# A two-group mixer layer on one core: order of the row scales, the embedding sums, the mixing weight and the gate tiles

## The chip, the core and the metric

The kernel runs on one core of a Trainium2 chip. The metric is the device time of one execution in microseconds. The core has a matrix engine (TensorE, PE in the rows, with its weight loads as PEld), a vector engine (VectorE, DVE), a scalar engine (ScalarE, ACT), a general engine (GpSimd, POOL) and an engine that here only issues DMAs (SyncE, SP). Each engine takes its instructions in one fixed order, and waits on semaphores where an instruction needs what another engine or a DMA makes.

## The reference

One layer (the stack has depth 1) on x of 1024 positions by 1024 features, all in float32:

```
h = rms_norm(x, pre_norm_gain)
q, k, v, z_a, b, c, u, z_c = split(h @ w_in, 8)          # 512 columns each
lam = exp(sum(lq1*lk1)) - exp(sum(lq2*lk2)) + 0.2
# group A: 4 heads, two softmax maps per head, ALiBi bias, block-causal mask
attn = rms_norm((softmax(q1 k1) - lam * softmax(q2 k2)) @ v, subln_gain) * 0.8 * silu(z_a)
# group B: depthwise convolution of width 3
conv = b * conv3(c * u) * silu(z_c)
x = x + rms_norm(concat(attn, conv) @ w_out, post_norm_gain)
e = rms_norm(p @ w_ple_proj, ple_norm_gain)              # p: 1024 by 256
out = x + sigmoid(x @ w_ple_gate) * e
```

## The kernel before

Everything is held transposed, features on the 128 partitions and positions along the free dimension, in two halves of 512 positions. Each float32 matrix product is made of three passes (lines 94 to 96): operands are split into a high part (ScalarE, line 83 or 86) and a low part (VectorE, or GpSimd for most weights, line 84 or 87). A product tile of 128 features by 512 positions takes 24 matmuls of 512 columns.

The order in which each engine gets its instructions is not the order of the text. The program is built with a scheduler that simulates the engines: among the instructions that are ready it prefers what stands earlier in the text, and it fixes one order per engine. A tile pool with a tag hands its few buffers round, so an instruction can also be late because a buffer isn't free.

The stages, with the names that matter here:

- **Embedding.** `embed(n, p)` makes e = p @ w_ple_proj for half n in 8 tiles `ple`, and stores them to DRAM (`e_dram`) through SP. Around it x is loaded (`load_x`), split into `hT`, and the weight tiles `wq`, `wk` of head 0 are loaded.
- **Row scales.** `row_scale(n)` finds 1/rms of x for half n: seven squares on ScalarE (`sqx`) added up on VectorE into `R[n]`, a transpose `flip` and a reduction `part` on VectorE, a small matmul `ms` on TensorE (line 110, in a PSUM bank of tag "t", which the `ple` tiles use too), a power on GpSimd (`rsx`, line 91), and a transpose that spreads the result into `R[n]` (line 114). Four copies then put the same numbers into `r_col`, by which v is scaled. `sqx`, `flip` and the temporaries `tq`, `ql`, `tk` of q and k share three buffers (pool `rowp`, tag "t").
- **Head 0's q, k, z and all of v.** `run` multiplies a weight tile with one half or both, and its evacuation (`ev_q`, `ev_k`, `ev_z`) multiplies the PSUM bank by `R[n]`. Half 1 of q and k has banks of its own (`bank_s`); z and v use the two banks of `bank_p`. v needs `r_col`. In the text `row_scale(1)` stands between the two halves of q and k.
- **Mixing weight.** `mixing_weight()` (lines 156 to 163) loads the four lambda vectors, broadcast over the partitions, into part of a buffer of x (`mix[5][1]`), and needs two products, two reductions, an exponential and two more small operations. In the text it stands behind v.
- **Heads.** For each head the list `PLAN` says the order of the steps: 'a' softmax blocks, 'v' reload v, 'g' `values` (transposes `tpw`, splits `wt`, products `av`, then a square on ScalarE, line 265, and column sums), 'n' `scale_values`, 'c' tiles of the convolution group, which fill TensorE, and 's' `embed_scale(n)` in heads 0 and 1.
- **Embedding sums.** `embed_scale(n)` (lines 429 to 441) reads back the eight tiles of e for half n into `mix[7]`, `mix[6]` and `mix[3]` (the last two in turn), squares each on ScalarE (line 436), adds it on GpSimd (line 438), and makes a column sum with `flip`, `part`, `ms` and a power. Its loads, squares and adds need nothing of the heads.
- **Output.** `out_half` makes the mixed tiles, `post(n, r)` norms them, adds x (by GpSimd for seven of eight tiles) and splits the sum into `x1[n]`. `gate_half(m, n)` loads e (three buffers), scales it (line 546), makes one gate tile from `x1[n]`, and ScalarE's tanh (line 555), a multiplication (line 556), an addition (line 557) and a store follow. In the text `post(1)` follows `gate_half(0, 0)`; then come gate tiles 1 to 4 of half 0, tiles 0 to 4 of half 1, and the rest in pairs.

Of the kernel before, what the change touches and what calls it, by code (L numbers as in the profile page):

```python
# [43 lines left out]
def hybrid_layer(ctx, tc, xT, pT, w_in, small, lams, w_out, w_ple, w_gate, outT):  # L44
# [103 lines left out]
    with ExitStack() as st:  # L148
        qk = st.enter_context(tc.tile_pool(name="qk", bufs=1))
        rowp = st.enter_context(tc.tile_pool(name="rowp", bufs=3))  # L150

        lam_in = mix[5][1][:, 0:256].rearrange("p (a b) -> p a b", a=4)
        lam_e = qk.tile([P, 2], F32, name="lam_e")
        nlam = qk.tile([P, 1], F32, name="nlam")

# [13 lines left out]
        class Head:  # L169
# [81 lines left out]
            def values(s, g):  # L251
                r0 = s.r0
                av = ps_a.tile([P, HALF], F32, tag="a", name="av")
                nj = 4 * g + 4
                for j in range(nj):
                    i0 = max(0, j - 4 * g)
                    tp = bank_t("tpw")
                    for ii in range(i0, 4):
                        T.transpose(out=tp[:, ii * P:(ii + 1) * P], in_=s.ws[ii][:, j * P:(j + 1) * P], identity=ident)  # L259
                    wt = a3.tile([P, 2, HALF], F32R, tag="wt", name="wt")  # L260
                    c = slice(i0 * P, HALF)
                    split(wt[:, 0, c], wt[:, 1, c], tp[:, c])
                    mm3(av[:, c], s.vs[:, 0, j], s.vs[:, 1, j], wt[:, 0, c], wt[:, 1, c], j == 0, j == nj - 1)
                sq = ap.tile([P, HALF], F32, tag="sq", name="sq")
                A.activation(out=sq, in_=av, func=AF.Square)
                o = mix[s.h][g]
                V.tensor_tensor(out=o, in0=av, in1=o, op=mult)
                ms = column_sums(sq, ap, extra=r0)
                rb = tiny.tile([P, 16], F32, tag="rb", name="rb")
                rs = tiny.tile([P, 16], F32, tag="rs", name="rs")  # L270
                V.tensor_copy(out=rb, in_=ms[:, 16:32])
                V.tensor_tensor(out=rs, in0=ms[:, 0:16], in1=rb, op=mult)
                V.tensor_tensor(out=rs, in0=rs, in1=rb, op=mult)
                rsqrt(rs, rs, P, 1e-5)
                V.tensor_tensor(out=rs, in0=rs, in1=rb, op=mult)
                s.rs[g] = rs
# [8 lines left out]
        with ExitStack() as st0:  # L285
            sp = st0.enter_context(tc.tile_pool(name="sp", bufs=1))
            s2 = st0.enter_context(tc.tile_pool(name="s2", bufs=2))

            wph = sp.tile([P, KT, 2, P], F32R, name="wph")
            wpo = sp.tile([P, KT, 2, P], F32R, name="wpo")  # L290

            splits = {}

            def load_x(n):
                for kt in range(KT):
                    nc.sync.dma_start(out=mix[kt][n], in_=xT[n, kt])
                    splits[n, kt] = split(hT[n][kt][:, 0], hT[n][kt][:, 1], mix[kt][n], col(C_PRE, kt))

            def load_ple(c):
                raw = rawp.tile([P, c.stop - c.start, 2, P], F32, tag="raw", name="rawe")  # L300
                nc.sync.dma_start(out=raw, in_=w_ple[:, c])
                split(wph[:, c], wpo[:, c], raw)

            def load_p(n):
                pth = s2.tile([P, 2, HALF], F32R, tag="pth", name="pth")
                pto = s2.tile([P, 2, HALF], F32R, tag="pto", name="pto")
                raw = rawp.tile([P, 2, HALF], F32, tag="raw", name="rawt")
                for k in range(2):
                    nc.sync.dma_start(out=raw[:, k], in_=pT[:, n, k])
                    split(pth[:, k], pto[:, k], raw[:, k])  # L310
                return pth, pto

            def embed(n, p):
                pth, pto = p
                for m in range(KT):
                    ps = bank_t("ple") if m % 3 else ps_a.tile([P, HALF], F32, tag="a", name="ple")
                    for k in range(2):
                        mm3(ps, wph[:, m, k], wpo[:, m, k], pth[:, k], pto[:, k], k == 0, k == 1)
                    e = s2.tile([P, HALF], F32, tag="e", bufs=5, name="e")
                    if m % 2:  # L320
                        A.copy(out=e, in_=ps)
                    else:
                        V.tensor_copy(out=e, in_=ps)
                    nc.sync.dma_start(out=e_dram[n, m], in_=e)


            zero = sp.tile([P, HALF], mybir.dt.bfloat16, name="zero")
            V.memset(zero, 0.0)
            idle = bank_p("idle")
            for _ in range(9):  # L330
                T.matmul(out=idle, lhsT=zero[:, :P], rhs=zero, start=True, stop=True)
            load_ple(slice(0, 1))
            pt0 = load_p(0)
            load_ple(slice(1, 4))
            load_ple(slice(4, 8))
            pt1 = load_p(1)
            embed(0, pt0)
            nc.sync.dma_start(out=sm, in_=small)
            V.tensor_scalar(out=subg, in0=sm[:, C_SUB:C_SUB + 1], scalar1=0.4, scalar2=None, op0=mult)
            load_x(0)  # L340
            embed(1, pt1)
            wq = w_in_tile(0, 0, V)
            wk = w_in_tile(1, 0, V)
            load_x(1)


        with ExitStack() as st0:
            vp = st0.enter_context(tc.tile_pool(name="vp", bufs=1, reuse_waits="tile"))
            v2 = st0.enter_context(tc.tile_pool(name="v2", bufs=2, reuse_waits="tile"))
            r_col = qk.tile([P, NT], F32, name="r_col")  # L350

            def sums_x(n):
                acc = R[n]
                A.activation(out=acc, in_=mix[0][n], func=AF.Square)
                for kt in range(1, KT):
                    sq = rowp.tile([P, HALF], F32, tag="t", name="sqx")
                    A.activation(out=sq, in_=mix[kt][n], func=AF.Square)
                    V.tensor_tensor(out=acc, in0=acc, in1=sq, op=add)
                return acc

            def row_scale(n):
                r = tiny.tile([P, 16], F32, tag="rs", name="rsx")
                rsqrt(r, column_sums(sums_x(n), rowp, tag="t")[:, :16], D, 1e-6)
                spread(R[n], r)
                for g in range(4):
                    V.tensor_copy(out=r_col[32 * g:32 * g + 32, 4 * n:4 * n + 4], in_=r[32 * g:32 * g + 32, g:16:4])

            head0 = Head(0)
            row_scale(0)
            run([(wq, head0.ev_q), (wk, head0.ev_k)], (0,))  # L370
            row_scale(1)
            run([(wq, head0.ev_q), (wk, head0.ev_k)], (1,), bank_s)
            run([(w_in_tile(3, 0), head0.ev_z)])
            wv = vp.tile([P, 2, KT, HALF], F32R, name="wv")
            for h in range(H):
                raw = rawp.tile([P, KT, P], F32, tag="raw", name="raw")
                nc.sync.dma_start(out=raw, in_=w_in[8 + h])
                c = slice(h * P, (h + 1) * P)
                split(wv[:, 0, :, c], wv[:, 1, :, c], raw)
            for j in range(NT):  # L380
                c = slice(j % 4 * P, j % 4 * P + P)
                ps = bank_p("v")
                for kt in range(KT):
                    b = hT[j // 4][kt]
                    mm3(ps, b[:, 0, c], b[:, 1, c], wv[:, 0, kt], wv[:, 1, kt], kt == 0, kt == KT - 1)
                v = v2.tile([P, 2, HALF], F32R, tag="v", name="v")
                split(v[:, 0], v[:, 1], ps, r_col[:, j:j + 1])
                nc.sync.dma_start(out=v_dram[j], in_=v.bitcast(F32))
            mixing_weight()
        ap = st.enter_context(tc.tile_pool(name="ap", bufs=1, reuse_waits="tile"))  # L390
        a2 = st.enter_context(tc.tile_pool(name="a2", bufs=2, reuse_waits="tile"))
        a3 = st.enter_context(tc.tile_pool(name="a3", bufs=3, reuse_waits="tile"))
# [61 lines left out]
        for h in range(H):  # L454
# [5 lines left out]
            for step in PLAN[h]:  # L460
# [8 lines left out]
                elif k == "g":  # L469
                    hd.values(int(v))  # L470
                elif k == "n":
                    hd.scale_values(int(v))
                elif k == "c":
                    conv_tiles(int(v))
                elif k == "s":
                    embed_scale(int(v))
                elif k == "t":
                    conv_tiles(int(v), together=True)


    with ExitStack() as st:
# [86 lines left out]
        r = post_stat(1)  # L568
        gate_half(0, 0)
        post(1, r)  # L570
        for m in range(1, 5):
            gate_half(m, 0)
        for m in range(0, 5):
            gate_half(m, 1)
        for m in range(5, 8):
            gate_half(m, 0)
            gate_half(m, 1)

# [36 lines left out]
```

## Time and profile before

| what | value |
|---|---|
| median of 3 runs | 669.23 us (667.34 to 671.49) |
| the profiled execution, its own time | 670.35 us |
| its span, first to last instruction | 668.5 us |
| mean granted TensorE clock | 0.992 |
| TensorE busy | 651.3 us, 97% of the span |
| VectorE, ScalarE, GpSimd busy | 454.6, 241.7 and 228.3 us |

The span is 1.9 us shorter than the execution's own time. A busy time is a sum over the span; where it is missing is seen in windows of the span and in the list of waits.

### The profile page before, as it was taken

To read this page: it belongs to the slowest core of one execution; us is meant where nothing else is said; L and a number is where in the kernel's file an instruction comes from. 1 tells how busy PE (TensorE), PEld (TensorE's weight loads), DVE (VectorE), ACT (ScalarE), POOL (GpSimd) and SP (SyncE) were. 2 spreads that over 40 slices of the span, in tenths; PEclk is the share of its full clock that TensorE was granted. 3 is DMA by queue.
4 is the path that set the end of the run, shared out by engine and by line. 5 is a ranking of instruction groups with operands and counts; after the bars stand their busy time and mean duration, and the time that the engine had idled before them with its cause. 6 is when DMAs were issued, how large, how long until landed. Compare 5 with 4: busy or idle time off the path is not lost.

```text
span 668.5 us, 8063 instructions
## 1 busy us (share of the span) xinstructions
PE 651.3 (97%) x2941; PEld 526.7 (79%) x2941; DVE 454.6 (68%) x828; ACT 241.7 (36%) x434; POOL 228.3 (34%) x115
## 2 busy tenths in 40 slices
PE   8999699999999999999999999999999999999996
PEld 5787478888888888888888888888888888877885
DVE  6959661479778786598834989618792189796333
ACT  6934441243443332344323334312541227231111
POOL 2046340032622354152351312425370187560000
PEclk9999899999999999999999999999999999999998
DMA  8966562300135001250012610113141024142222
GB/s 289 403 223 188 183 202 94 127 32 32 48 85 152 32 31 49 54 151 33 33 63 51 169 33 32 50 32 108 63 158 32 1 94 163 57 132 91 96 94 94
DMA packets 35654, 67.77 MB, mean 101 GB/s; under 512 B 3744, under 2 KB 12448, under 8 KB 35616
## 3 DMA queue, kind: packets, MB, share of 16 engines
q1 hardware_dynamic: 35616, 67.27, 30.7%
q8 instruction: 23, 0.38, 0.2%
q14 instruction: 15, 0.12, 0.1%
HBM read 48.38 MB, written 12.58 MB: 91 GB/s over the span
## 4 chain that ended last, share of the span: by engine, by line
PE 67%; DMA 11%; DVE 10%; issue 6%; POOL 5%; ACT 1%; SPq 0%; DVEq 0%; POOLq 0%
PE pj L94 12%; PE pj L96 12%; PE pj L95 12%; PE o L94 5%; PE o L96 5%; PE o L95 5%; PE s L232 5%; DMA e<-e_dram 4%; DMA out_dram<-e 3%; PE tpw L259 2%; POOL w L84 2%; PE v L94 2%; PE v L95 2%; PE v L96 2%; DMA mix<-in_xT 2%
## 5 line engine op out<-in xcount | busy, mean ns | idle before, releaser
L94 PE MATMUL pj<-hT,w 128*128 128x512 f32 x448 | 179.1, 400 | 0.6 <-ACT w L83 0.4
L96 PE MATMUL pj<-hT,w 128*128 128x512 f32 x448 | 178.1, 398 | 0.0
L95 PE MATMUL pj<-hT,w 128*128 128x512 f32 x448 | 177.9, 397 | 0.0
L84 POOL TENSOR_TENSOR w<-raw,w 128x1024 fp32r<-128x1024 f32 x42 | 106.8, 2549 | 202.3 <-ACT w L83 190.4
L94 PEld LDWEIGHTS pj<-hT,w 128*128 128x128 f32 x448 | 84.3, 188 | 19.3 <-ACT w L83 0.8
L96 PEld LDWEIGHTS pj<-hT,w 128*128 128x128 f32 x448 | 84.2, 188 | 18.6
L95 PEld LDWEIGHTS pj<-hT,w 128*128 128x128 f32 x448 | 84.2, 188 | 18.0
L240 ACT ACTIVATE p<-p,nm 128x128 f32<-128x128 f32 (+7 forms) x64 | 49.4, 772 | 73.9 <-DVE nm L236 63.3
L83 ACT CAST w<-raw 128x1024 fp32r<-128x1024 f32 x44 | 45.8, 1047 | 51.3 <-issue 35.2
L95 PE MATMUL o<-x,w 128*128 128x512 f32 (+1 forms) x136 | 52.1, 383 | 1.5 <-DVE x L84 1.5
L94 PE MATMUL o<-x,w 128*128 128x512 f32 (+1 forms) x136 | 52.2, 385 | 0.0
L96 PE MATMUL o<-x,w 128*128 128x512 f32 (+1 forms) x136 | 51.9, 381 | 0.0
L94 PE MATMUL o<-mT,w 128*128 128x512 f32 x128 | 51.1, 399 | 0.0
L96 PE MATMUL o<-mT,w 128*128 128x512 f32 x128 | 50.4, 395 | 0.0
L95 PE MATMUL o<-mT,w 128*128 128x512 f32 x128 | 50.2, 392 | 0.0
L232 PE MATMUL s<-ks,qs 128*128 128x512 f32 (+2 forms) x192 | 46.6, 347 | 0.5 <-issue 0.5
L236 DVE CUSTOM_DVE_ANT_0 p<-s,bias 128x512 f32<-128x512 f32 (+3 forms) x64 | 34.7, 565 | 9.6 <-PE s L232 5.6
L546 DVE SCALAR_TENSOR_TENSOR e<-e,sm,re 128x512 f32<-128x512 f32 x16 | 16.2, 1015 | 35.9 <-DMA e<-e_dram 35.9
L232 PEld LDWEIGHTS s<-ks,qs 128*128 128x128 f32 x192 | 33.3, 188 | 6.2 <-issue 0.9
L83 ACT CAST wt<-tpw 128x512 fp32r<-128x512 f32 (+3 forms) x48 | 20.7, 478 | 45.1 <-PE tpw L259 44.9
L84 DVE TENSOR_TENSOR wt<-tpw,wt 128x512 fp32r<-128x512 f32 (+3 forms) x48 | 25.2, 551 | 16.4 <-ACT wt L83 16.1
L555 ACT ACTIVATE tg<-o 128x512 f32<-128x512 f32 (+1 forms) x17 | 9.7, 572 | 65.6 <-PE o L96 63.0
(139 smaller groups left out, 1134.0 us busy)
## 6 DMA issues: line engine op xcount, KB each, us to landing
raw<-in_w_in SPq DMA_DIRECT2D x32, 512.0 KB, 3.9
mix<-in_xT SPq DMA_DIRECT2D x16, 256.0 KB, 5.9
e_dram<-e SPq DMA_DIRECT2D x16, 256.0 KB, 5.2
mix<-e_dram SPq DMA_DIRECT2D x16, 256.0 KB, 3.5
ks<-ks SPq DMA_DIRECT2D x16, 256.0 KB, 3.6
v_dram<-v SPq DMA_DIRECT2D x8, 512.0 KB, 3.1
vs<-v_dram SPq DMA_DIRECT2D x32, 128.0 KB, 2.8
raw<-in_w_out SPq DMA_DIRECT2D x8, 512.0 KB, 3.3
```

The source lines that it names most:

```text
L83: A.copy(out=hi, in_=src)
L84: (lo_eng or V).tensor_tensor(out=lo, in0=src, in1=hi.bitcast(F32), op=sub)
L94: T.matmul(out=ps, lhsT=ah, rhs=bh, start=first, stop=False)
L95: T.matmul(out=ps, lhsT=ah, rhs=bl, start=False, stop=False)
L96: T.matmul(out=ps, lhsT=al, rhs=bh, start=False, stop=last)
L232: T.matmul(out=banks[m][:, :nn], lhsT=s.qs[:, m, qi], rhs=s.ks[:, m, part, c], start=part == 0, stop=part == 1)
L236: V.tensor_tensor_reduce(out=pr[m][:, c0:c0 + n], in0=banks[m][:, :n], in1=s.bias[:, b0:b0 + n], scale=-1.0, scalar=low[m], op0=add, op1=A ...
L240: A.activation(out=pr[m][:, :W], in_=pr[m][:, :W], func=AF.Exp, scale=-1.0, bias=low[m], accum_out=l[:, m:m + 1])
L259: T.transpose(out=tp[:, ii * P:(ii + 1) * P], in_=s.ws[ii][:, j * P:(j + 1) * P], identity=ident)
L546: V.scalar_tensor_tensor(out=e, in0=e, scalar=col(C_PLE, m), in1=re[n], op0=mult, op1=mult)
L555: A.activation(out=t, in_=ps, func=AF.Tanh, scale=0.5)
```

## The change

The row scale of half 1 is written ahead of both halves of q and k. The copies to `r_col` go from VectorE to ScalarE. The low part of head 0's z weight is made by VectorE in place of GpSimd. The mixing weight is written into the embedding stage, with the conv group's buffer `gt` (not used until the first conv tile) for its input in place of a buffer of x. `embed_scale` stands in the plan where it stood, but its instructions on ScalarE are queued behind the square of the head's last `values` (`issue_after` fixes an issue order on that engine; it adds no wait, and SP, GpSimd and VectorE are not bound by it). The gate tiles of half 0 that run ahead of half 1's are six in place of five.

```diff
-        lam_in = mix[5][1][:, 0:256].rearrange("p (a b) -> p a b", a=4)
+        lam_in = gt[:, 0:256].rearrange("p (a b) -> p a b", a=4)
...
-                A.activation(out=sq, in_=av, func=AF.Square)
+                s.last = A.activation(out=sq, in_=av, func=AF.Square)
...
             embed(1, pt1)
+            mixing_weight()
             wq = w_in_tile(0, 0, V)
...
-                    V.tensor_copy(out=r_col[32 * g:32 * g + 32, 4 * n:4 * n + 4], in_=r[32 * g:32 * g + 32, g:16:4])
+                    A.copy(out=r_col[32 * g:32 * g + 32, 4 * n:4 * n + 4], in_=r[32 * g:32 * g + 32, g:16:4])
...
             row_scale(0)
+            row_scale(1)
             run([(wq, head0.ev_q), (wk, head0.ev_k)], (0,))
-            row_scale(1)
             run([(wq, head0.ev_q), (wk, head0.ev_k)], (1,), bank_s)
-            run([(w_in_tile(3, 0), head0.ev_z)])
+            run([(w_in_tile(3, 0, V), head0.ev_z)])
...
-            mixing_weight()
...
                 elif k == "s":
-                    embed_scale(int(v))
+                    with tc.issue_after(hd.last.ins):
+                        embed_scale(int(v))
...
-        for m in range(1, 5):
+        for m in range(1, 6):
             gate_half(m, 0)
-        for m in range(0, 5):
+        for m in range(0, 6):
             gate_half(m, 1)
-        for m in range(5, 8):
+        for m in range(6, 8):
             gate_half(m, 0)
             gate_half(m, 1)
```

## Rows read from the trace of the kernel before

**Rows 1.** Busy time in windows: length, each engine's busy time (instructions), clock, DMA.

```profile
13.00:25.00 12.00, 11.18 (x46) 8.19 (x45) 11.61 (x20) 11.83 (x21) 0.00 (x0) 1.00 1.04 399
...
56.00:73.97 17.97, 17.42 (x75) 13.66 (x74) 15.43 (x14) 9.83 (x15) 7.49 (x4) 1.00 0.67 202
73.97:89.20 15.23, 8.87 (x32) 6.58 (x30) 9.57 (x19) 4.82 (x9) 10.29 (x6) 0.78 0.55 187
...
204.00:285.00 81.00, 81.00 (x388) 66.83 (x387) 59.60 (x128) 27.55 (x49) 30.04 (x14) 1.00 0.19 56
...
598.00:607.00 9.00, 7.50 (x30) 4.80 (x29) 9.00 (x12) 3.00 (x6) 2.98 (x2) 1.00 0.33 103
607.00:668.50 61.50, 55.84 (x263) 45.87 (x262) 23.04 (x37) 6.75 (x12) 0.00 (x0) 0.97 0.30 99
```

**Rows 2.** Who TensorE waited for, whole span: total, times, longest.

```profile
PE ms L110 <- DVE part L103: 3.2, 1, 3.2
PE v L94 <- DVE v L87: 2.6, 1, 2.6
PE o L95 <- DVE x L84: 1.5, 2, 0.7
```

**Rows 3.** Windows again, of the instructions on v alone.

```profile
68.33:73.86 5.53, 5.53 (x24) 4.40 (x24) 0.00 (x0) 0.00 (x0) 1.00 0.79 227
73.97:89.20 15.23, 7.77 (x26) 5.91 (x25) 0.74 (x1) 0.67 (x1) 0.78 0.55 187
```

**Rows 4.** Timeline of VectorE: start, duration, instruction, idle time before it.

```profile
50.64 0.71 DVE L114 STREAM_TRANSPOSE R<-rsx 128x512 f32<-128x512 f32 x1 [1.65 <-POOL rsx L91]
...
74.84 0.36 DVE L159 TENSOR_TENSOR mix<-mix 128x64 f32<-128x64 f32 x2 [2.88 <-DMA mix<-in_lams]
...
79.66 0.74 DVE L87 SCALAR_TENSOR_TENSOR v<-v,r_col 128x512 fp32r<-128x512 f32 x1
84.96 0.71 DVE L114 STREAM_TRANSPOSE R<-rsx 128x512 f32<-128x512 f32 x1 [4.55 <-POOL rsx L91]
```

**Rows 5.** Timeline of ScalarE, same columns.

```profile
66.89 1.67 ACT L357 ACTIVATE sqx<-mix 128x512 f32<-128x512 f32 x3 [3.06 <-DVE ks L84]
...
72.32 0.63 ACT L436 ACTIVATE mix<-mix 128x512 f32<-128x512 f32 x1 [1.28 <-DMA mix<-e_dram]
75.48 0.63 ACT L436 ACTIVATE mix<-mix 128x512 f32<-128x512 f32 x1 [2.52 <-DMA mix<-e_dram]
```

**Rows 6.** Embedding sums by line: waits of the squares, adds (min/median/max ns), loads.

```profile
  DMA mix<-e_dram: 13.5, 9
...
L438 POOL TENSOR_TENSOR mix<-mix,mix x14: 1264/1296/1761, 34.6 to 96.2; 128x512 f32<-128x512 f32 x14
...
DMA to landing us min/median/max: 2.6/3.5/7.0
```

**Rows 7.** Timelines of ScalarE and TensorE in heads 0 and 1.

```profile
203.70 0.60 ACT L265 ACTIVATE sq<-av 128x512 f32<-128x512 f32 x1 [0.55 <-PE av L96]
...
217.77 0.29 PE L110 MATMUL ms<-part,fold 128*128 128x16 f32 x2
...
219.53 0.57 ACT L83 CAST wt<-tpw 128x512 fp32r<-128x512 f32 x1
...
224.12 0.39 PE L94 MATMUL av<-wt,vs 128*128 128x512 f32 x1
```

**Rows 8.** Timelines of VectorE and ScalarE among the gate tiles.

```profile
606.15 0.68 DVE L84 TENSOR_TENSOR x<-mix,x 128x512 fp32r<-128x512 f32 x1
...
637.16 0.68 DVE L557 TENSOR_TENSOR e<-e,mix 128x512 f32<-128x512 f32 x1
...
640.32 0.60 ACT L555 ACTIVATE tg<-o 128x512 f32<-128x512 f32 x1 [5.00 <-PE o L96]
...
642.60 0.75 DVE L546 SCALAR_TENSOR_TENSOR e<-e,sm,re 128x512 f32<-128x512 f32 x1 [4.15 <-DMA e<-e_dram]
643.27 0.68 DVE L557 TENSOR_TENSOR e<-e,mix 128x512 f32<-128x512 f32 x1
```

## The prediction, made before the changed kernel was seen

> **What bounds the kernel now.** I read the page first: TensorE is busy 651.3 of 668.5 us, so only its 17 us of idle time and its slow clock can be won. Then the waits of TensorE: two of 3.2 and 2.6 us stand at single places and one of 1.5 us at another [rows 2]. Then windows, to see what each place costs. From 73.97 to 89.20 us TensorE is busy 8.87 of 15.23 us at a clock of 0.78 (part of it at 1.2 GHz, after the two idle times) [rows 1]; before it a tile of v ran 24 matmuls in 5.53 us, 0.230 each [rows 3]. The stretch holds 26 matmuls of v (5.98 us at that pace) and 6 small ones (0.15 each by the pair `ms`, two in 0.29 us [rows 7]: 0.9). So it takes 15.23 - 5.98 - 0.9 = **8.3 us too long**. From 598 to 607 us 1.5 us are idle, and in heads 0 and 1 nothing is: 81.00 of 81.00 [rows 1].
>
> Then back from the 8.3 us by the timelines. The first wait is for `part` of half 1's row scale. Half 1's squares ran only at 66.89 us, when a buffer came back from k's low parts [rows 5]; the last addition stood in VectorE's queue behind the mixing weight's first product, which waited 2.88 us for its load [rows 4]. The second is for the low part of the first v tile at 79.66 us, behind the rest of the mixing weight; ScalarE, which makes the high part, had stood 2.52 us for a load of the embedding sums [rows 4, 5]. `R[1]` was spread only at 84.96 us, against 50.64 for `R[0]` [rows 4], and until then z's second bank isn't free, so v goes through one bank. Three of the five edits take away one of these causes each.
>
> **The change part by part.** Base: the profiled execution's 670.35 us (668.5 of span and 1.9 around it); it is 1.1 above the median, which I take off at the end.
>
> *Row scale of half 1 ahead of q and k.* Nothing is added. Seven squares, seven additions, `flip`, `part`, `ms`, power and spread move ahead of buffers that wait for `R[0]`. VectorE has little room before 25 us (11.61 of 12.00 [rows 1]), but x is loaded in the embedding stage, and TensorE has work without any row scale (embedding, q and k of both halves) beyond 50.64 us, where `R[0]` is spread now [rows 4]. `ms` of half 1 needs a bank of the embedding's tiles, which `ms` of half 0 needs too; a second power on GpSimd follows the first, so `R[1]` should come some 4 us behind `R[0]` (a spread waited 4.55 us for its power [rows 4]), near 55 us, and z and v then run on two banks. With the next two edits this gives back the 8.3 us: **-8.3**. Ends: -6.4, the idle time alone, if the clock still drops (15.23 - 8.87), and -9.1, with the 0.55 us idle just before it (17.97 - 17.42 [rows 1]) and 0.25 for the restarts behind the waits. What is late next: the evacuations of q and k of half 1 now crowd those of half 0 ahead of z and v; VectorE was busy 15.43 of 17.97 us there [rows 1]. The 0.55 us already lost there I leave as it is; if the four extra evacuations came in front of z's, it would grow by up to about 3.
>
> *Mixing weight in the embedding.* Its load joins SP's queue ahead of `wq`, `wk` and half 1 of x, and six small operations join VectorE's, where evacuations of `ple`, the splits of `hT` and the low parts of `wq` wait behind them. VectorE is 97% busy from 13 to 25 us [rows 1], so about 1 us of it (two products in 0.36 us, as many reductions, the rest small) is pushed on, and if the load is late VectorE stands as it did for 2.88 us [rows 4]. Between 0 and 3.9; TensorE already waits there for evacuations (11.18 of 12.00), but three banks lie between, so I take **+0.5**.
>
> *Embedding sums behind the last values.* Sixteen squares and fourteen additions of 1.30 us leave the stretch from 34.6 to 97 us [rows 6] for heads 0 and 1, and with them the loads from the fourth on of each half: the first three have free buffers, the others wait for an addition, and SP's queue holds them. ScalarE stood 13.5 us for these loads in nine places [rows 6]; now what is queued behind such a wait is `wt` and the exponentials. The cover: `wt` is ready at 220.10 us and TensorE takes it at 224.12, so 4.0 us of delay cost nothing [rows 7]. A load lands in 3.5 us as a median but 7.0 at most [rows 6]. GpSimd has room (30 of 81 us). TensorE also gets two `ms` in a fixed place, and waits there if the sums come late. Below 0 I see nothing in a stretch without idle time; up to 16 if both `ms` come early (below). I take **+0.8**.
>
> The additions took 1.26 to 1.76 us [rows 6], so something stretches some of them. A rule speaks against moving them: the Trainium skill, "SBUF — State Buffer", section "Who interferes with whom", has GpSimd and a VectorE operation with two SBUF inputs share one port pair, and the later one is blocked for the whole operation. By it 7 x 1.30 = 9.1 us of each half's additions would come on top of VectorE's 59.60 of 81 us [rows 1]. The stretched additions agree with it; a blocked VectorE is what the second rival below is made of.
>
> *Copies to `r_col` on ScalarE, z's low part on VectorE.* Eight small copies and one low part change engine; VectorE loses eight small operations and gains a large one. **0**: TensorE's work without a row scale covers both; without that cover the low part's own time would show.
>
> *Six gate tiles in the first sweep.* TensorE lost 1.5 us to `x1` of half 1 [rows 1, 2], whose last low part ends at 606.83 [rows 8]. One tile more of half 0 is 5.60 us of cover (5.00 + 0.60 between two tanh, the pace of TensorE [rows 8]), so that wait goes. But the end isn't set there: an addition at 637.16 is followed by the next at 643.27, 6.11 us later, and what stands between is a store, a load of e and its scaling, for which VectorE waits 4.15 us [rows 8]. This chain is slower than TensorE and runs from about 606 us to the end, behind the same `post(1)` work. So most of the 1.5 us comes back as waiting: **-0.3**, between -3.1 (the wait, restarts and the lag of the chain all gone) and +1.
>
> Sum: -8.3 + 0.5 + 0.8 - 0.3 = -7.3. 670.35 - 7.3 = 663.05 by the profiled execution, less 1.1: **661.9 us**, likely between 659.5 and 664.5.
>
> **Rivals.** *The gate edit pays and the crowding goes.* If VectorE's new order makes the additions before the next scaling, the chain breaks: -3.1 in place of -0.3, and the 0.55 and half of the costs go too: about 657. Against it: the edit touches neither the number of e buffers nor `post(1)`.
>
> *The sums cost in the heads what they cost before.* An addition that blocks VectorE (1.30) and a load (3.5) fall together: 4.8 against a cover of about 4.0, 0.8 for each gated load, ten loads of which half hit something: +4. With the wider waits of up to 7.0 us, about 666. For it: 13.5 us of such waits; against it: no idle time in heads 0 and 1.
>
> *The row scale doesn't come early.* If `ms` of half 1 sits in TensorE's queue where VectorE isn't ready, TensorE waits there as it waits now; the stall only moves, perhaps to 45 us, and half of the 8.3 is saved: 666.
>
> *Slower: TensorE waits for the sums.* `ms` of half 0's sum ran at 217.77 us, 14.1 us after the square at 203.70 [rows 7], when the adds were long done. The eight steps of half 1's sum went from 72.32 us to the last add at 96.2 + 1.3 [rows 5, 6], 25 us. If `ms` keeps its place while five gated loads follow the square (5/8 of 25 = 16, at worst 25), TensorE stands 2 to 11 us, twice; at 6.5 each, and with 1.6 us for a clock that falls as it fell before (26 v matmuls took 7.77 busy us in place of 5.98), that is +16: 678. It decides from a chain of 14 us on, less what the order allows for.
>
> **How the numbers follow.** Forecast 0.55, gate edit pays 0.13, heads 0.16, row scale 0.10, slower 0.06. About 1%, 6.7 us, is what a measurement of this kernel tells from no change: the line is at 662.5. Of the forecast's 0.55, 0.41 lie under it; with the 0.13 that is 0.54 for faster. Within 1%: 0.14 + 0.16 + 0.10 = 0.40. Slower 0.06. The range for 8 in 10 goes from 656.5, the whole of the best case, to 667, past the two middling rivals.
>
> **What would show it.** Right: no TensorE wait over 1 us between 56 and 130 us, the clock at 1.0 there, `R[1]` spread before 60 us, the gap between additions of gate tiles still near 6.1 us. Wrong: `ms` waits of several us in heads 0 and 1 or near 45 us; idle time of TensorE from 13 to 25 us grown by over 1 us; a v tile that waits for a bank.

## The result, and the profile after

The changed kernel takes **660.63 us** (median of 4 runs, 659.43 to 661.79) against 668.79 for the kernel before beside it (4 runs): ratio **0.9873, 95% interval 0.9835 to 0.9912**, or 8.2 us less by the medians and 8.5 by the ratio. The forecast was 661.9, in a range from 656.5 to 667. The profiled executions lie further apart, 670.35 and 659.43, since that of before is above its median and that of after is the fastest of its four. In the rows of after, line numbers from 342 to 389, and from 477 on, are one higher than in before.

The page of after, span and busy time of each engine:

```profile
span 657.7 us, 8063 instructions
...
PE 644.0 (98%) x2941; PEld 523.8 (80%) x2941; DVE 447.0 (68%) x821; ACT 243.2 (37%) x442; POOL 229.3 (35%) x114
```

Windows of after, columns as in [rows 1]:

```profile
13.00:25.00 12.00, 9.99 (x40) 7.01 (x40) 12.00 (x24) 12.00 (x23) 0.00 (x0) 1.00 1.04 399
...
56.00:73.97 17.97, 17.97 (x80) 14.61 (x79) 15.76 (x17) 9.60 (x14) 8.01 (x3) 1.00 0.73 214
73.97:89.20 15.23, 15.23 (x71) 12.69 (x70) 1.50 (x2) 1.40 (x3) 0.00 (x0) 1.00 0.31 126
204.00:285.00 81.00, 81.00 (x387) 66.76 (x387) 62.00 (x139) 33.73 (x67) 38.96 (x21) 1.00 0.25 75
...
60.00:80.00 20.00, 20.00 (x90) 16.43 (x89) 12.93 (x13) 7.08 (x11) 6.41 (x3) 1.00 0.61 186
...
598.00:607.00 9.00, 9.00 (x40) 7.23 (x39) 3.45 (x6) 1.20 (x2) 0.00 (x0) 1.00 0.46 147
```

The stretch that held the stall is full: 15.23 of 15.23 us at clock 1.00, where before had 8.87 at 0.78 [rows 1]. So is the one before it. The heads, which took the sums, are still full, and the 1.5 us of waits for `x1` are gone from TensorE's list of waits. Of these windows only 13 to 25 us got worse, by 1.2 us of TensorE.

Who TensorE waited for in after, the longest two, in place of the 3.2 and 2.6 us of [rows 2]:

```profile
PE idle L331 <- DVE zero L328: 1.2, 1, 1.2
PE pj L94 <- ACT w L83: 1.1, 2, 0.7
```

Timeline of VectorE in after, to set against [rows 4] and [rows 8] (columns: start, duration, instruction, idle time before it):

```profile
50.97 0.70 DVE L114 STREAM_TRANSPOSE R<-rsx 128x512 f32<-128x512 f32 x1
54.44 0.70 DVE L114 STREAM_TRANSPOSE R<-rsx 128x512 f32<-128x512 f32 x1
...
60.32 4.23 DVE L84 TENSOR_TENSOR ks<-tk,ks 64x512 fp32r<-64x512 f32 x2 [0.61 <-ACT ks L83]
...
65.20 0.68 DVE L211 TENSOR_TENSOR mix<-pj,R 128x512 f32<-128x512 f32 x1
...
68.01 1.41 DVE L84 TENSOR_TENSOR ks<-tk,ks 64x512 fp32r<-64x512 f32 x2
69.44 0.69 DVE L211 TENSOR_TENSOR mix<-pj,R 128x512 f32<-128x512 f32 x1
...
644.11 0.75 DVE L547 SCALAR_TENSOR_TENSOR e<-e,sm,re 128x512 f32<-128x512 f32 x1 [4.26 <-DMA e<-e_dram]
644.78 0.68 DVE L558 TENSOR_TENSOR e<-e,mix 128x512 f32<-128x512 f32 x1
...
650.18 0.75 DVE L547 SCALAR_TENSOR_TENSOR e<-e,sm,re 128x512 f32<-128x512 f32 x1 [4.11 <-DMA e<-e_dram]
650.85 0.68 DVE L558 TENSOR_TENSOR e<-e,mix 128x512 f32<-128x512 f32 x1
...
654.03 0.42 DVE L558 TENSOR_TENSOR e<-e,mix 128x256 f32<-128x256 f32 x1
```

`R[1]` comes at 54.44 us, 3.5 us behind `R[0]` (before 84.96). Both evacuations of z (line 211) are done by 70.1 us. One pair of low parts, at 60.32 us, still takes 4.23 us where the next takes 1.41: GpSimd is busy beside it with its own low parts of weights (58.41 to 64.02 us). TensorE doesn't wait for it here. The gate tiles still follow one another at 6.07 us (644.78 to 650.85).

Where the time went, by the starts of TensorE's first and last matmul on v and of its first gate matmul, and the end of the span (us; e4 runs the same program as before up to the gate, e5, e6 and e12 the same as after):

| | first v | last v | first gate | end |
|---|---|---|---|---|
| before | 68.33 | 121.90 | 570.17 | 668.49 |
| e4, gate edit alone | 67.13 | 119.57 | 567.84 | 666.57 |
| after | 66.69 | 110.78 | 558.71 | 657.65 |
| e5, e6, e12 | 67.24, 67.01, 67.29 | 111.33, 111.10, 111.39 | 559.33, 559.03, 559.51 | differ |

From first to last v it is 53.57 us in before and 52.44 in e4, and 44.09 or 44.10 in all four kernels with the new order: **8.3 to 9.5 us won in this stretch**. Ahead of it about 0.7 us is won (means 67.73 and 67.06). From last v to the first gate matmul it is 448.27 in both before and e4, and 447.93 to 448.12 in the other four. From there to the end it is 98.32 and 98.73 against 98.94 for after: 0.2 to 0.6 lost.

### The profile page after: what moved, and what is told of

Same layout as the page of the kernel before. It is cut to its first block, busy times and chain, and to the rows that moved or that the text cites. A ratio compares the mean times of both kernels' runs of the same rounds, so it can differ in the third digit from the quotient of the medians.

```text
span 657.7 us, 8063 instructions
## 1 busy us (share of the span) xinstructions
PE 644.0 (98%) x2941; PEld 523.8 (80%) x2941; DVE 447.0 (68%) x821; ACT 243.2 (37%) x442; POOL 229.3 (35%) x114
## 4 chain that ended last, share of the span: by engine, by line
PE 83%; DMA 8%; DVE 6%; issue 1%; ACT 1%; SPq 0%; DVEq 0%
PE pj L96 16%; PE pj L95 16%; PE pj L94 16%; PE s L232 5%; PE o L95 5%; PE o L96 5%; PE o L94 5%; DMA e<-e_dram 4%; DMA out_dram<-e 3%; PE tpw L259 2%; PE v L95 2%; PE v L96 2%; PE v L94 2%; DVE e L558 2%; PE av L96 1%; PE av L95 1%
## 5 line engine op out<-in xcount | busy, mean ns | idle before, releaser
L401 POOL TENSOR_TENSOR mix<-mix,R 128x512 f32<-128x512 f32 x8 | 11.5, 1436 | 75.9 <-DVE mix L400 73.8
```

Source lines behind the costliest of these rows:

```text
L401: G.tensor_tensor(out=o, in0=o, in1=R[n], op=mult)
```

## The experiments

The prediction's theory, **A**, is that half 1's late row scale, waiting in queues behind loads and buffers, is the root of the stall in the v stretch, and that each of three edits takes away a cause of its own. **Rival B** has the stall as the sum of queues behind two late loads, that of the mixing weight and those of the embedding sums, whatever the place of the row scale. For the gate, the prediction has the chain of store, load of e and scaling set the end, not TensorE.

All ratios are to the kernel before, run beside it on the same chip. The interval of after itself is 5 us wide, so a difference of less than about 2.5 us from after is read from the traces, and not from the medians alone.

| | median us | ratio, 95% interval |
|---|---|---|
| e1 before + row scale early | 667.72 | 0.9989 [0.9976, 1.0001] |
| e2 before + mixing weight early | 666.50 | 0.9965 [0.9949, 0.9981] |
| e3 before + sums late | 663.66 | 0.9926 [0.9899, 0.9953] |
| e4 before + gate edit | 671.35 | 1.0030 [1.0010, 1.0050] |
| e5 after + six e buffers | 655.79 | 0.9808 [0.9792, 0.9824] |
| e6 after - gate edit | 659.34 | 0.9862 [0.9846, 0.9878] |
| e7 after, sums early again | 670.00 | 1.0009 [0.9994, 1.0024] |
| e8 after, mixing weight late again | 662.96 | 0.9911 [0.9889, 0.9934] |
| e9 as e7, without the additions | 661.11 | 0.9876 [0.9856, 0.9896] |
| e10 as e7, without the squares | 668.58 | 0.9999 [0.9985, 1.0013] |
| e11 after, row scale late again | 663.43 | 0.9912 [0.9893, 0.9931] |
| e12 as e6, with six e buffers | 658.11 | 0.9833 [0.9815, 0.9852] |

**e1, the row scale alone.**

```diff
             row_scale(0)
-            run([(wq, head0.ev_q), (wk, head0.ev_k)], (0,))
             row_scale(1)
+            run([(wq, head0.ev_q), (wk, head0.ev_k)], (0,))
```

> The kernel before with one edit: half 1's row scale ahead of q and k. Theory A (the late row scale is the root: half 1's squares waited for buffers that wait for half 0's scale, and z's second bank waited for the result): the stretch of 8.3 us falls to 1 to 3 us, the time falls by 5 to 8 us, half 1's scale is spread before 65 us. Rival B (the stall is the sum of queues behind two late loads, the mixing weight's and the embedding sums'): the row scale alone saves under 3 us, and ScalarE and VectorE still stand for those loads while TensorE waits.

Nothing that can be told from no change, although the edit did what it says: `R[1]` was spread at 60.48 us. TensorE now stands once, for longer. Its waits, and then the timelines of VectorE and of GpSimd, in e1:

```profile
PE v L94 <- ACT qs L83: 5.9, 1, 5.9
```
```profile
63.52 3.32 DVE L84 TENSOR_TENSOR wv<-raw,wv 128x1024 fp32r<-128x1024 f32 x1
66.76 4.49 DVE L84 TENSOR_TENSOR ks<-tk,ks 64x512 fp32r<-64x512 f32 x2
...
71.89 0.68 DVE L211 TENSOR_TENSOR mix<-pj,R 128x512 f32<-128x512 f32 x1
```
```profile
63.01 6.03 POOL L84 TENSOR_TENSOR w<-raw,w 128x1024 fp32r<-128x1024 f32 x2 [0.62 <-ACT w L83]
69.00 3.38 POOL L438 TENSOR_TENSOR mix<-mix,mix 128x512 f32<-128x512 f32 x2
```

For the wait the profile names a cast of half 1's q, which v doesn't read. What v needs is one of the two banks that it shares with z, and z's first evacuation (line 211, 71.89 us) ends just ahead of v's start at 72.71 us. That evacuation takes its usual 0.68 us; it is late because the low parts ahead of it took 7.8 us. With GpSimd idle the same ones take 2.6 (e9, below). GpSimd was busy all the while, with its own low parts of weights and then with the additions of the embedding sums. Theory A falls: an early row scale alone gives next to nothing.

**e2, the mixing weight alone.**

```diff
-        lam_in = mix[5][1][:, 0:256].rearrange("p (a b) -> p a b", a=4)
+        lam_in = gt[:, 0:256].rearrange("p (a b) -> p a b", a=4)
...
             embed(1, pt1)
+            mixing_weight()
...
-            mixing_weight()
```

> The kernel before with one edit: the mixing weight in the embedding stage. Theory A: the 2.88 us that VectorE stood for its load are gone, so the first wait (3.2 us) shrinks and the second with it, but half 1's squares still run after 62 us and z's second bank stays late: -2 to -4 us in all. Rival B: the load was the cause, -5 us or more. The cost that I gave the edit in the embedding (+0.5 us) would show as idle time of TensorE from 13 to 25 us, 1 us or more over before.

2.3 us less, as theory A has it (2 to 4) and not Rival B (5 or more). TensorE's waits for the row scale and for v shrink to 1.1 us for v, but it now also stands once for 2.7 us ahead of the scores, until 83.80 us. The profile names nothing for it; it ends just behind the evacuation of half 1's q (line 189, 83.00 to 83.69 us), which stands behind the late `R[1]`, spread at 80.1 us, and its copies.

**e3, the sums alone.**

```diff
-                A.activation(out=sq, in_=av, func=AF.Square)
+                s.last = A.activation(out=sq, in_=av, func=AF.Square)
...
                 elif k == "s":
-                    embed_scale(int(v))
+                    with tc.issue_after(hd.last.ins):
+                        embed_scale(int(v))
```

> The kernel before with one edit: the squares of the embedding sums behind the square of the head's last values. Theory A: ScalarE no longer stands for these loads near 75 us, the second wait (2.6 us) shrinks, -1 to -3 us; in heads 0 and 1 TensorE stays without idle time. Rival B: -3 us or more. The rival of the prediction in which the sums cost in the heads what they cost before: TensorE idle 2 us or more from 200 to 320 us.

5.0 us less, the largest of the three and more than theory A had for it (1 to 3), with the row scale still late (`R[1]` at 76.1 us, itself 9 us earlier than before). TensorE's waits in the stretch fall to these:

```profile
PE v L94 <- DVE v L87: 1.3, 1, 1.3
PE ms L110 <- DVE part L103: 0.9, 1, 0.9
```

**e7, all of the change but the sums,** which is e3's edit taken out of after.

```diff
...
                 elif k == "s":
-                    with tc.issue_after(hd.last.ins):
-                        embed_scale(int(v))
+                    embed_scale(int(v))
```

> The changed kernel without the queueing of the embedding sums. If the late row scale was the root: the sums may run early again at little cost, 0 to +2 us, with ScalarE's waits for loads back between 30 and 100 us. Rival B: 3 us or more slower, with TensorE waiting for ScalarE or VectorE between 60 and 90 us.

The whole gain is gone: 1.0009. Windows, waits of TensorE, VectorE and GpSimd in e7:

```profile
60.00:80.00 20.00, 14.82 (x60) 11.37 (x59) 19.02 (x15) 9.51 (x15) 15.95 (x8) 0.96 0.76 215
```
```profile
PE v L94 <- DVE mix L211: 5.2, 2, 3.7
```
```profile
57.37 0.70 DVE L114 STREAM_TRANSPOSE R<-rsx 128x512 f32<-128x512 f32 x1
...
63.63 3.99 DVE L84 TENSOR_TENSOR ks<-tk,ks 64x512 fp32r<-64x512 f32 x2
67.65 0.69 DVE L211 TENSOR_TENSOR mix<-pj,R 128x512 f32<-128x512 f32 x1
...
74.57 2.72 DVE L213 SCALAR_TENSOR_TENSOR mix<-tz,mix 128x512 f32<-128x512 f32 x1
77.21 0.68 DVE L211 TENSOR_TENSOR mix<-pj,R 128x512 f32<-128x512 f32 x1
```
```profile
65.33 1.74 POOL L438 TENSOR_TENSOR mix<-mix,mix 128x512 f32<-128x512 f32 x1
67.03 2.83 POOL L84 TENSOR_TENSOR w<-raw,w 128x1024 fp32r<-128x1024 f32 x1
69.83 3.45 POOL L438 TENSOR_TENSOR mix<-mix,mix 128x512 f32<-128x512 f32 x2
73.99 2.75 POOL L84 TENSOR_TENSOR w<-raw,w 128x1024 fp32r<-128x1024 f32 x1 [0.71 <-ACT w L83]
```

From 60 to 80 us VectorE is busy 19.02 us and GpSimd 15.95, against 12.93 and 6.41 in after. The second evacuation of z starts at 77.21 us, not 69.44, and v waits 3.7 us for its bank. `R[1]` was there at 57.37, so it isn't the row scale. By the traces 7.5 of the 9.4 us between the medians of e7 and after are lost at the last v (118.31 us against 110.78).

The sums bring two kinds of work, and e9 and e10 part them. **Theory C**: GpSimd's additions hold up VectorE. **Theory D**: the squares on ScalarE and their loads hold up ScalarE, which makes the high parts.

**e9, e7 without the fourteen additions.**

```diff
                 A.activation(out=e, in_=e, func=AF.Square)
-                if m:
-                    G.tensor_tensor(out=acc, in0=acc, in1=e, op=add)
```

> The changed kernel with the embedding sums early again (the run that lost the whole gain), and with GpSimd's fourteen additions left out, so that the statistic is that of one tile. Loads and squares stay. Theory C (the additions hold VectorE up between 50 and 80 us, so that z's evacuation comes late and TensorE waits for its bank): the waits of v for z's evacuation (5.2 us) and the lowered clock go, the last v matmul comes 6 us or more earlier than with the additions, the time is 660 to 663 us. Theory D (ScalarE's squares and their waits for loads do it): the stall stays, 667 us or more.

The gain is back (0.9876) with the sixteen squares and loads still early, so it wasn't Rival B's late loads either. The last v starts at 111.05 us, 7.3 earlier than in e7. Windows and VectorE in e9:

```profile
60.00:80.00 20.00, 20.00 (x90) 16.45 (x89) 13.56 (x14) 10.45 (x16) 8.06 (x3) 1.00 1.00 271
```
```profile
58.31 1.22 DVE L84 TENSOR_TENSOR wv<-raw,wv 128x1024 fp32r<-128x1024 f32 x1
59.45 1.40 DVE L84 TENSOR_TENSOR ks<-tk,ks 64x512 fp32r<-64x512 f32 x2
```

**e10, e7 without the squares,** but for one of each sum.

```diff
-                A.activation(out=e, in_=e, func=AF.Square)
                 if m:
                     G.tensor_tensor(out=acc, in0=acc, in1=e, op=add)
+            A.activation(out=acc, in_=acc, func=AF.Square)
```

> The changed kernel with the embedding sums early again, and with ScalarE's squares left out but for one square of each sum, so that the statistic is not the reference's. Loads and GpSimd's additions stay. Theory C: the stall of v on z's evacuation stays, at 3 us or more, 666 us or more. Theory D: it goes, 660 to 663 us.

Nothing is back (0.9999). Waits, windows and GpSimd in e10:

```profile
PE v L94 <- DVE mix L211: 5.4, 1, 5.4
```
```profile
60.00:80.00 20.00, 14.61 (x60) 11.55 (x59) 19.06 (x14) 9.12 (x12) 18.48 (x9) 0.91 0.82 252
```
```profile
56.75 10.01 POOL L437 TENSOR_TENSOR mix<-mix,mix 128x512 f32<-128x512 f32 x5
```

VectorE beside them:

```profile
59.88 3.49 DVE L84 TENSOR_TENSOR ks<-tk,ks 64x512 fp32r<-64x512 f32 x2
```

In the changed order theory C holds and D falls. Five additions in a row took 10.01 us, 2.0 each, where the median of one is 1.30 [rows 6], and the low parts beside them 3.49 us where e9 has 1.40: the two engines stretch each other. Additions and squares were not parted in the order of before.

**e8, the mixing weight late again.**

```diff
-        lam_in = gt[:, 0:256].rearrange("p (a b) -> p a b", a=4)
+        lam_in = mix[5][1][:, 0:256].rearrange("p (a b) -> p a b", a=4)
...
             embed(1, pt1)
-            mixing_weight()
...
+            mixing_weight()
```

> The changed kernel with the mixing weight back behind v. If the late row scale was the root: nothing waits there on half 1's sums, so 0 to +1 us, or up to 1 us faster if the embedding loses what the edit put into it (the +0.5 us of the prediction, seen as idle time of TensorE from 13 to 25 us). Rival B: 3 us or more slower.

Its median is 2.3 us above after's, with intervals that overlap and six runs from 659.99 to 665.48. In its trace, the fastest run, one wait of 1.0 us stands before v and the last v starts at 111.86 us, 0.5 to 1.1 later than in the four kernels of the table. That is between the two theories (0 to 1, and 3 or more) and not settled.

**e11, the row scale late again.**

```diff
             row_scale(0)
-            row_scale(1)
             run([(wq, head0.ev_q), (wk, head0.ev_k)], (0,))
+            row_scale(1)
```

> The changed kernel with half 1's row scale between the halves of q and k again; sums late, mixing weight early. If the row scale's place matters once the additions are away: its spread comes after 70 us, v waits 1 to 3 us for a bank or for the column sum, the time is 2 to 4 us above the changed kernel. If the additions alone made the stall: within 1 us of the changed kernel.

2.8 us above after's median. `R[1]` came at 74.7 us, TensorE waited 1.3 us for v's low part, and the last v started at 112.77, 1.4 to 2.0 later than in the table. The trace also has 2.1 us more than after from the first gate matmul to the end (101.00 against 98.94), which is the chain of the gate tiles and not the row scale (below, at the gate edit). So the row scale's place is worth 1.4 to 2.0 us once the additions are gone, and less than can be told while they are there (e1).

**e4 and e6, the gate edit alone, and all but the gate edit.** e6 undoes in after what e4 does in before:

```diff
-        for m in range(1, 5):
+        for m in range(1, 6):
             gate_half(m, 0)
-        for m in range(0, 5):
+        for m in range(0, 6):
             gate_half(m, 1)
-        for m in range(5, 8):
+        for m in range(6, 8):
...
```

> The kernel before with one edit: six gate tiles of half 0 ahead of half 1. Theory A (the end is set by the chain of store, load of e and scaling on VectorE): TensorE's 1.5 us of waits for the split of half 1 are gone and its last matmul ends about 2.5 us earlier against the first gate tile, but the last addition does not: time within 1 us of before. Rival (TensorE sets the end): -2.5 us.

> The changed kernel with five gate tiles in the first sweep again. By the chain that sets the end: within 0.7 us of the changed kernel, although TensorE waits 1.5 us more for the split of half 1. Rival (the sixth tile is worth what TensorE gained, 2.5 us): 2 to 3 us slower than the changed kernel.

e4 is 2.0 us slower than before, where theory A had it within 1 us. TensorE's gate work did get shorter: from its first gate matmul to the end of its last it is 92.67 us in before and 90.13 in e4. The end didn't follow: 98.32 and 98.73 us from the first gate matmul. e6 has the wait for `x1` again (1.3 us in two pieces) and still takes 98.46 to the end, 0.5 less than after; the two medians, 659.34 and 660.63, have intervals that overlap.

**e5, after with more e buffers.**

```diff
-            e = c4.tile([P, HALF], F32, tag="e", bufs=3, name="e")
+            e = c4.tile([P, HALF], F32, tag="e", bufs=6, name="e")
```

> The changed kernel with six buffers for e in the gate stage in place of three, so that a load of e no longer waits for a store of three tiles before. If the chain of store, load and scaling sets the end of the changed kernel: the waits of VectorE for e (4 us for each tile) go, the last addition follows TensorE's last matmul by 1 to 2 us, and the time falls by 2 to 3.5 us against the changed kernel (about 12% of a per cent: ratio to before 0.983). If the end is set by TensorE or by the last stores: no change beyond 0.5 us.

4.8 us less than after, 655.79, the fastest kernel here, and more than was expected (2 to 3.5). Why is seen in SyncE's timeline of after:

```profile
645.49 0.34 SPq L559 DMA_DIRECT2D out_dram<-e  x1
647.53 0.32 SPq L546 DMA_DIRECT2D e<-e_dram  x1
```

A load of e goes out 2.04 us after the store from its buffer, and its scaling starts 2.65 us later, at 650.18 us; meanwhile VectorE, whose queue goes in order, stands 4.11 us, although the tanh of the tile that is scaled there (of its first piece) had started at 646.16 us and took 0.39. In e5 VectorE and ScalarE end like this:

```profile
644.40 0.69 DVE L557 SCALAR_TENSOR_TENSOR e<-tg,e 128x512 f32<-128x512 f32 x1 [4.18 <-ACT tg L556]
...
650.39 0.42 DVE L558 TENSOR_TENSOR e<-e,mix 128x256 f32<-128x256 f32 x1
```
```profile
649.52 0.38 ACT L556 ACTIVATE tg<-o 128x256 f32<-128x256 f32 x1 [2.49 <-PE o L96]
```

VectorE now waits for the tanh and the tanh for TensorE. The last tanh of a tile starts 0.04 us after TensorE's last gate matmul ends (649.48), in after 3.4 us (652.23 and 648.86).

**e12, five tiles in the first sweep and six buffers.**

> The changed kernel with six buffers for e and five gate tiles in the first sweep. With the chain of store and load broken, TensorE sets the end, so here the sixth tile must show what it is worth: TensorE waits 1.5 us for the split of half 1 and restarts, 2 to 3 us slower than the run with six buffers and six tiles (655.8), 657.5 to 659. If the sixth tile is worth nothing at all: 655.8 within 0.7.

658.11, 2.3 us more than e5. TensorE waits for `x1`, and now this shows:

```profile
PE o L95 <- DVE x L84: 1.5, 3, 0.7
```

So the sixth tile is worth 2.3 us where TensorE sets the end (e5 against e12), and nothing, or a small loss, where the chain does (after against e6, e4 against before).

## Why the prediction was right, and where it was not

The time was right, 661.9 against 660.63, and so was the size of its main term. The reason given for that term was not. That the size came out all the same is partly luck: the 8.3 us was measured as what the stretch lost, whatever the cause, and the edit that takes away the cause nobody had named was one of the three. All four signs that the prediction gave for "right" came, and none of them tells which edit did it.

- **Row scale, mixing weight and sums, -8.3.** Measured: 8.3 to 9.5 us between first and last v. The step that failed is the sentence "Three of the five edits take away one of these causes each". The causes it names, half 1's squares without buffers, the load of the mixing weight in VectorE's queue, and ScalarE's 2.52 us wait for a load of the sums, are what the waits named last. Under them lay one that stands in the same windows and was not used: GpSimd was busy 7.49 and 10.29 us in the two windows [rows 1], and VectorE's operations with two SBUF inputs beside it were slow. These rows of VectorE's timeline of before show it:

```profile
59.29 2.94 DVE L84 TENSOR_TENSOR ql<-tq,qs 64x512 fp32r<-64x512 f32 x1
62.26 4.60 DVE L84 TENSOR_TENSOR ks<-tk,ks 64x512 fp32r<-64x512 f32 x2
...
77.32 2.16 DVE L162 TENSOR_TENSOR nlam<-lam_e 128x1 f32<-128x1 f32 x1
```

  The first takes 0.68 us in after and the second 1.40 in e9; the 3.06 us that half 1's squares waited [rows 5] last until the second is done. The third works on one column and takes 0.16 us in e1. Here it ends at 79.48 us together with the low part of GpSimd in the next row, and v's low part, whose high part was ready at 78.61 us, stood behind it:

```profile
77.12 2.35 POOL L84 TENSOR_TENSOR w<-raw,w 128x1024 fp32r<-128x1024 f32 x1 [10.81 <-ACT w L83]
```

  GpSimd's work there is its own low parts of weights as well as the additions, and the rows don't part the two. The pair of low parts takes 3.90 us in e3 and 4.23 in after, without any addition, and after's GpSimd is busy 8.01 us in the first window while TensorE is full. That it was the additions that made the stall is shown by taking them away, and not by these rows.

  The runs give the sums 5.0 us alone (e3), and with them early again the other edits win nothing (e7), because of the additions (e9, e10). The row scale is worth under 2 us alone by e1's interval, and 1.4 to 2.0 after the sums by e11's trace; the mixing weight 2.3 alone (e2), and 0.5 to 1.1 after the sums by e8's trace. The edits don't add: an early row scale moves the evacuations of half 1 into the time of the additions, and TensorE's wait goes from `part` and v's low part (5.8 us) to a bank for v (5.9).
- **The late row scale as a sign.** The spread of `R[1]` at 84.96 us [rows 4] was taken for a cause. In e3 it comes at 76.1 with its place unchanged, so part of its lateness was VectorE's own.
- **A rule put to the wrong place.** The Trainium skill, "SBUF — State Buffer", section "Who interferes with whom", has a GpSimd operation that reads SBUF and a VectorE operation with two SBUF inputs exclude each other. The prediction held it against the sums' new place. The traces agree with it where the sums came from: two low parts of 64x512 took 1.40 us with GpSimd idle (e9) and 3.99 to 4.60 beside it (e7, after, e1, before), and the subtraction of one column in before ended together with GpSimd's low part. Operations that read PSUM and one SBUF tile (lines 189 and 211) kept to 0.69 beside it; they are late only because they queue behind the others.
- **Mixing weight in the embedding, +0.5.** The sign given for "wrong" did come: TensorE's idle time from 13 to 25 us grew by 1.2 us. With the mixing weight late (e8) it is 10.51 busy of 12.00, so 0.5 of the growth is its. But v didn't start later; it started some 0.7 us earlier. Part of that is the run: a matmul of `ple` (line 94) took 446 ns as a mean in before's profile and 406 in after's, and 409 and 431 in e1 and e3, whose embedding is before's.
- **Sums in the heads, +0.8.** Measured: nothing, 0.2 to 0.3 us less from last v to the first gate matmul. ScalarE does stand for the loads, longer than before, as its rows in after show (loads: total wait and times), and the additions keep their 1.30 us:

```profile
L436 ACT ACTIVATE mix<-mix x16: 619/632/634, 193.0 to 301.8; 128x512 f32<-128x512 f32 x16
...
  DMA mix<-e_dram: 21.3, 9
...
L438 POOL TENSOR_TENSOR mix<-mix,mix x14: 1291/1300/1769, 194.3 to 302.5; 128x512 f32<-128x512 f32 x14
```

  TensorE is busy 81.00 of 81.00 us all the same, and waits nowhere in the heads. The longest of these waits, 5.49 us, ends at 214.75 us; the next `wt` isn't held up by it but waits another 3.71 us for TensorE's transposes. So the rivals that have TensorE stand for the loads or for the sums (666 and 678) fall.
- **Copies and z's low part, 0.** Not tried by itself. In after z's low part takes VectorE 1.21 us at 35.48, with no wait of TensorE.
- **The gate edit, -0.3.** Right in kind: the chain sets the end, as e5 and e12 show by breaking it. The size was +0.2 to +0.6 by the traces, and e4's runs have it at +2.0 (interval 0.7 to 3.3). The traces have a part of that loss. From the first gate matmul to the end it is 98.09 to 98.46 us in the five kernels with five tiles and three buffers (before, e1, e2, e3, e6), and 98.33 to 101.00 in the seven with six (e8, e4, after, e10, e9, e7, e11, in this order). In the chain one store, that of the eleventh gate tile, makes most of the difference: the load behind it goes out 2.04 us after it in e8, 2.33 to 2.48 in after, e4 and e10, and 3.41, 3.68 and 3.92 in e9, e7 and e11; in the five kernels it is 2.03 or 2.04 at the same place. Why this store is slow in some executions stays open. The rival in which it pays needed the chain broken, which only the buffers do.
- **Row scale not early (666).** It was early, at 54.44 us, as forecast ("near 55 us").
- **A sum among the rivals.** The first rival's "about 657" comes to 658 by its own terms: 661.9 less 2.8, 0.55 and 0.65.

## What to carry to other kernels

When evacuations come late, look at whether the operations ahead of them in VectorE's queue take longer than elsewhere in the trace, and at what GpSimd runs beside them, before the wait that is named last: work on GpSimd that nobody needs yet can cost TensorE time in a stretch where VectorE is nearly full (19.02 of 20 us in e7), and nothing in one where VectorE has room (62.00 of 81 in after's heads). Edits to one stall need not add (here they don't), so the one to be tried alone is the removal of load from the engine that is full, and an early operand helps only after it. A buffer that goes store, load, next use on an engine that works in order is a chain with a period of its own; set it against the pace of the engine that is to lead, and give it buffers before reordering that engine's work.

## What the runs showed of the hardware beyond the forecast

- Fourteen additions of GpSimd, 18 us of its time at 1.30 each, cost 8.9 us of the whole kernel (e7 against e9): a pair of VectorE's low parts took 3.49 us beside them where it takes 1.40 alone (e10, e9), and the additions themselves 2.0 us each in a row of five (e10).
- TensorE lost on top of its waits: behind the 3.7 us wait in e7 matmuls of v come 0.43 us apart in place of 0.23, with the granted clock at the lower of its two levels (1.2 GHz; 0.50 from 80 to 81 us) and 0.96 as a mean from 60 to 80 us; in e10, behind 5.4 us, it is 0.91. In after there is no such wait in the stretch and the clock is 1.00.
- The load of e behind the store of its buffer had a period of 5.97 to 6.44 us a tile in after, over eight tiles, against 5.60 for TensorE [rows 8]. Its stores didn't all take the same: the one named above held up the load behind it for 2.04 to 3.92 us, from one kernel's trace to another's.
